# Softmax weights times values as three float32r products of high and low parts, the exponential taken twice

## The chip, the cores and the metric

The kernel runs on one NeuronCore of a Trainium2 chip. The metric is the device time of one execution in microseconds (us). Beside it stands the profile of one execution: for each engine (TensorE for matrix products, VectorE, ScalarE, GpSimd, and SyncE, which here only issues DMAs) the instructions with their start, their duration and what they waited for.

## The reference

One step of a one-layer hybrid encoder, for a prompt of 2048 tokens and for 8 streams of 16 new tokens with 512 cached ones. A combined input projection feeds two groups of heads: an SSD (state space) group and an attention group with forget gates. Their outputs go through one output projection, then a convolutional feed-forward network and a final norm. The change touches the attention of the prompt:

```python
def fox_block(q, k, v, fq, fk, q_pos, k_pos):
    s = jnp.einsum('bqhd,bkhd->bhqk', q, k).astype(jnp.float32) * FOX_SCALE
    s = s + (jnp.swapaxes(fq, 1, 2)[:, :, :, None] - jnp.swapaxes(fk, 1, 2)[:, :, None, :])
    s = jnp.where((k_pos[None, :] <= q_pos[:, None])[None, None], s, -jnp.inf)
    p = jax.nn.softmax(s, axis=-1)
    return jnp.einsum('bhqk,bkhd->bqhd', p.astype(v.dtype), v)
```

All is float32: 8 heads of 64 columns, 2048 queries and keys, causal.

## The kernel before, in words

The program has three phases that overlap. Phase A projects the input in four parts of 512 tokens (`a_body`, from L378). The attention runs over the same four parts of 512 queries and over 8 heads. Then come the output projection (`out_proj`, L910) and the feed-forward network (`ffn_part`), which take the second half of the time and are not touched, apart from `out_proj`.

TensorE's order is written out by hand (the `manual_schedule` block near the end of `hybrid_step`); the other engines' orders are chosen by the scheduler from its own times. The main loop there walks through the attention's blocks. After each block it gives out credit, and with it steps of the projection of the next part (stages 0 to 2) or of the output projection (stages 3 and 4); besides it runs the steps of a side job: the sample attention during part 0, SSD chunks (`ssd_chunk`) during parts 1 to 3. So each attention block on TensorE is followed by some us of other products.

Attention has two halves that run as a pipeline. `s_phase` (L653) computes scores with queries on partitions and takes their maxima (L668, L671), one head ahead. `t_phase` (L701) computes the scores again with keys on partitions, 128 keys by up to 512 queries a block: L728 and L729, both float32r products, and L731 for the mask on a diagonal block. ScalarE takes the exponential out of PSUM into the SBUF tile `pr` (L733), and two blocks later `weigh` (L695) multiplies it by the values (L696) into the PSUM tile `pv`. A part p has 8 heads of 4(p + 1) blocks, 320 in all; of the four blocks on the diagonal three are shorter (384, 256 and 128 queries).

L696 is a true float32 product. Its stationary operand, `vr` from `load_v` (L632), holds 64 columns of values and 64 columns of ones, so that one product gives the weighted sum and the softmax's denominator. For even heads the ones stand behind the values and for odd heads ahead of them. `end` copies both halves out of `pv` (L709, L710), and after two heads VectorE divides (`chores`: L713 in four pieces, L717).

Nearly everywhere else a float32 product is made of three float32r products. Float32r is a form of float32 in which a part of the digits is kept; `split` (L100) makes `hi`, the rounded number, and `lo`, what is left of it, and the product is hi x hi + hi x lo + lo x hi (`mm3`, L118).

The buffers that matter: PSUM tiles `s`, four of one bank each (`pss`), for the scores of both halves, the SSD chunks and the sample attention; one PSUM tile `pv`; three PSUM tiles `mm` for phase A; in SBUF five `pr`, three `v`, three `ks` (keys of `s_phase`), three `ev` (outputs of phase A on their way to memory), two `mx` (the split input of `out_proj`). SyncE issues all loads and stores but those of weights.

Of the kernel before, what the change touches and what calls it, by code (L numbers as in the profile page):

```python
# [8 lines left out]
F32 = mybir.dt.float32  # L9
# [8 lines left out]
P = 128  # L18
# [3 lines left out]
NB = 8  # L22
# [27 lines left out]
WB = 6  # L50
XB = 1
QB = 4
PB = 5
WA = 3
LEAD = 4

# [10 lines left out]
def hybrid_step(ctx: ExitStack, tc: tile.TileContext, i: dict, o: dict):  # L67
# [70 lines left out]
    def at(shape, tag, bufs, dt=F32):  # L138
        return ap_.tile(shape, dt, tag=tag, name=tag, bufs=bufs)
# [117 lines left out]
    def gates(p, dtf):  # L257
# [52 lines left out]
        V.tensor_copy(an[:, 0:8 * n].rearrange("p (c h) -> p c h", h=8), ct[:, 0, :, 0:8])  # L310
        pr = tpt()
        T.transpose(pr[0:8 * n, 0:P], an[:, 0:8 * n], ident)
        ar = at([40, P], "g_ar", 1)
        V.tensor_copy(ar[0:8 * n], pr[0:8 * n, 0:P])
        dS(ac_d[4 * p:4 * p + 4].rearrange("c h p -> (c h) p"), ar[0:32])
        if p == 0:
# [9 lines left out]
        for a in range(2):  # L326
            pr = tpt()
            for c in range(4):
                T.transpose(pr[0:8, c * P:(c + 1) * P], nh[:, a, c * 8:(c + 1) * 8].bitcast(F32), ident)
            fr = at([8, 512], "g_2k", 1)  # L330
            V.tensor_copy(fr, pr[0:8])
            dS(k2_d[:, 64 + a, p * 512:(p + 1) * 512], fr)
        yield
        if p > 0:
            return
# [16 lines left out]
        for c in range(4):  # L352
            V.scalar_tensor_tensor(snf[:, :, :, c], lcs[:, :, c, :], -1.0, cto, op0=ALU.mult, op1=ALU.subtract)
            V.tensor_add(cto, cto, ltt[:, :, c, :])
        snh = at([P, 2, 256], "g_2k", 1, F32R)
        split(snf.rearrange("p b h c -> p (b h c)"), snh[:, 0], snh[:, 1], V, V)
        yield
        pr = tpt()
        for a in range(4):
            T.transpose(pr[:, a * P:(a + 1) * P], snh[:, a // 2, (a % 2) * P:(a % 2 + 1) * P].bitcast(F32), ident)  # L360
        snr = at([P, 512], "xT", 2)
        V.tensor_copy(snr, pr)
        for a in range(4):
            dS(sf_d[a // 2, 4 * (a % 2):4 * (a % 2) + 4].rearrange("b h (c p) -> (b h c) p", p=P), snr[:, a * P:(a + 1) * P])
        ow8 = at([P, 8, NB], "g_ow8", 1)
        V.tensor_mul(ow8, cto.rearrange("p b h -> p h b"), blkb[:, None, :].to_broadcast([P, 8, NB]))
        ow = at([P, 8], "g_ow", 1)
        V.tensor_reduce(ow, ow8, op=ALU.add, axis=AX.X)
# [256 lines left out]
        return k12  # L625

    def load_ks(h, kb):
        ks = bt_([P, 512], "ks", 3, F32R)
        dma(ks[0:68].bitcast(F32), k2_d[h, :, kb * 512:(kb + 1) * 512])
        return ks  # L630

    def load_v(h, kb):  # L632

        vr = bt_([P, 4, P], "v", 3)
        e = h % 2 * HD
        G.memset(vr[:, :, HD - e:2 * HD - e], 1.0)
        dma(vr[:, :, e:e + HD], o["v"][4 * kb:4 * kb + 4, :, h * HD:(h + 1) * HD].rearrange("c p d -> p c d"))
        return vr

    def load_q(h, qb):  # L640
        q12 = bt_([P, 2, 512], "q12", QB, F32R)
# [51 lines left out]
    late, chores, exps = [], [], []  # L693

    def weigh(pv, vr, jj, of, pr, first, last, end):  # L695
        m = T.matmul(pv[:, of:512], vr[:, jj], pr[:, :512 - of], start=first, stop=last)  # L696
        pv_ins.append(m.ins)
        if last:
            end()

    def t_phase(h, qb, q12, yl, dn):  # L701

        pv = []
        order = [qb] + list(range(qb))

        def end():
            e = h % 2
            rs, ot = slice(e * 64, e * 64 + 64), slice(64 - e * 64, 128 - e * 64)
            S.copy(yl[rs], pv[0][rs])  # L709
            S.copy(dn[rs], pv[0][ot])  # L710
            if e:
                for a in range(4):
                    chores.append(lambda cc=slice(a * P, (a + 1) * P): V.reciprocal(dn[:, cc], dn[:, cc]))  # L713
                chores.append(norm)

        def norm():
            V.tensor_mul(yl, yl, dn)  # L717
            dS(mix_d[4 * qb:4 * qb + 4, :, 4 + h // 2, :].rearrange("c p t -> p c t"), yl.rearrange("p (c t) -> p c t", t=P))

        for kb in order:  # L720
            kk = load_k(h, kb)
            vr = load_v(h, kb)
            for jj in range(4):
                of = jj * P if kb == qb else 0
                W = 512 - of
                js = slice(jj * P, (jj + 1) * P)
                ps = pss()
                T.matmul(ps[:, :W], kk[:, 0, js], q12[:, 0, of:], start=True, stop=False)  # L728
                T.matmul(ps[:, :W], kk[0:68, 1, js], q12[0:68, 1, of:], start=False, stop=kb != qb)  # L729
                if kb == qb:  # L730
                    T.matmul(ps[:, 0:P], maskT, identb, start=False, stop=True)  # L731
                pr = bt_([P, 528], "pr", PB)
                exps.append(S.activation(pr[:, :W], ps[:, :W], AF.Exp).ins)  # L733
                first = kb == qb and jj == 0
                while len(late) >= (3 if late and late[0][0] == "first" else 2):
                    kind, a, x = late.pop(0)
                    if kind == "first":
                        a.append(psb.tile([P, 512], F32, tag="pv", name="pv", bufs=1))
                    weigh(a[0], *x)
                late.append(("first" if first else "", pv, (vr, jj, of, pr, first, kb == order[-1] and jj == 3, end)))  # L740
                yield
# [46 lines left out]
    def sample_attention():  # L788
# [33 lines left out]
        for b in range(NB):  # L822
# [38 lines left out]
            pT = bt_([P, 512], "pr", PB)  # L861
            S.copy(pT, pk)
            pk = pss()
            T.transpose(pk[0:NT, 0:P], pr[:, PAST:], ident)
            pt5 = bt_([NT, P], "bs", 1)
            V.tensor_copy(pt5, pk[0:NT, 0:P])
            yield
            pz = pss()
# [40 lines left out]

    def out_proj(c, after=None):  # L910
        mr = op.tile([P, KT, P], F32, tag="raw", name="raw", bufs=2)
        mx = op.tile([P, 2, KT, P], F32R, tag="mx", name="mx", bufs=2)

        for ks in ([slice(0, KT - 1), slice(KT - 1, KT)] if 12 <= c < 16 else [slice(0, KT)]):
            dA(mr[:, ks], mix_d[c][:, ks])
            split(mr[:, ks], mx[:, 0, ks], mx[:, 1, ks], S, V)
        y = op.tile([P, D], F32, tag="y", name="y", bufs=1)
        dA(y, i["xr"][c])
        ps = [pso.tile([P, 512], F32, tag="dn", name="dn") for _ in range(2)]

        def part(e, k):
            cc = slice(e * 512, (e + 1) * 512)
            T.matmul(ps[e], mx[:, 0, k], wo[k][:, 0, cc], start=k == 0, stop=False)  # L923
            T.matmul(ps[e], mx[:, 0, k], wo[k][:, 1, cc], start=False, stop=False)  # L924
            T.matmul(ps[e], mx[:, 1, k], wo[k][:, 0, cc], start=False, stop=k == KT - 1)  # L925
# [465 lines left out]
```

## Time and profile before

| | us |
|---|---|
| median of three runs | 3158.28 (3156.93 to 3160.4) |
| the profiled execution | 3159.18 |
| its span, first to last instruction | 3157.5 |
| mean granted clock of TensorE | 0.984 |

The profile's page lists busy time by engine, the chain of work that ended last, and groups of instructions by line, with the idle time of the engine ahead of them. A line of the kind `L733 ACT ACTIVATE pr<-s 128x512 ... x223 | 132.2, 595 | 202.3 <-PE s L729` says: line 733, ScalarE, reads `s` and writes `pr`, 223 times, busy 132.2 us together, 595 ns each, after 202.3 us in which ScalarE stood idle, mostly for TensorE. In the timeline the first number is the start and the second the duration, in us. A matmul's duration includes its way through the pipeline and its queue, so the time that one takes of TensorE is seen from start to start. A true float32 matmul leaves two records.

### The profile page before, as it was taken

The page shows a single profiled execution, that of the slowest core. Times are in us where ns is not written, and L with a number is a line of the kernel's source. Part 1 is how long each engine was busy: PE and PEld are TensorE (multiplying, and loading weights), DVE is VectorE, ACT ScalarE, POOL GpSimd, SP SyncE. Part 2 cuts the span into 40 slices and gives each one's busy share as a digit, 9 for nine tenths or more (in the row PEclk, how much of TensorE's full clock was granted, in tenths as well). Part 3 has the DMA queues.
Part 4 walks back from the last instruction along what each step waited for, and adds up shares of the span by engine and source line. Part 5 has one row for each costly group of instructions (what it writes and reads, how often), then busy time and mean ns, then how long its engine had stood idle before and what let it go on. Part 6 is the DMA issues. An engine that isn't in the chain of part 4 may idle for free.

```text
span 3157.5 us, 45849 instructions
## 1 busy us (share of the span) xinstructions
PE 3039.0 (96%) x17888; PEld 2682.1 (85%) x17888; DVE 1788.8 (57%) x3294; ACT 1066.7 (34%) x1927; POOL 865.8 (27%) x654
## 2 busy tenths in 40 slices
PE   7988998899999998999999999999999999999998
PEld 7886877787788775777899999999999999999998
DVE  4264466647565654543455555566555556766666
ACT  3343344444444444332322232233222223332322
POOL 3322322222222212000233232333223232433332
PEclk9998999899999999999999999999999999999999
DMA  4856675575556546445522121232121122322221
GB/s 123 247 174 202 200 244 158 181 223 165 162 155 204 153 132 187 161 148 181 171 67 67 54 69 61 72 116 79 61 67 61 60 67 83 105 67 81 74 69 65
DMA packets 233137, 395.77 MB, mean 125 GB/s; under 512 B 62544, under 2 KB 118488, under 8 KB 232920
## 3 DMA queue, kind: packets, MB, share of 16 engines
q1 hardware_dynamic: 181224, 238.41, 24.3%
q10 hardware_dynamic: 51696, 154.43, 15.8%
q8 instruction: 141, 2.31, 0.3%
q14 instruction: 76, 0.62, 0.1%
HBM read 314.51 MB, written 78.25 MB: 124 GB/s over the span
## 4 chain that ended last, share of the span: by engine, by line
PE 85%; DMA 8%; DVE 2%; ACT 2%; issue 1%; SPq 1%; POOL 1%; ACTq 0%; DVEq 0%; POOLq 0%
PE mm L120 11%; PE mm L121 11%; PE mm L122 11%; PE pv L696 6%; PE dn L1025 5%; PE dn L1026 5%; PE dn L1027 5%; PE mm L444 3%; PE mm L445 3%; PE mm L446 3%; DMA xt<-in_xr 2%; PE dn L923 2%; PE dn L925 2%; PE dn L924 2%; PE mm L397 2%; PE mm L399 2%
## 5 line engine op out<-in xcount | busy, mean ns | idle before, releaser
L105 POOL TENSOR_TENSOR wr<-raw,wr 128x1024 fp32r<-128x1024 f32 x198 | 476.5, 2415 | 1032.5 <-ACT wr L102 1024.5
L120 PE MATMUL mm<-nT,wr 128*128 128x386 f32 (+1 forms) x2112 | 696.4, 330 | 1.3 <-ACT wr L102 0.8
L121 PE MATMUL mm<-nT,wr 128*128 128x386 f32 (+1 forms) x2112 | 695.3, 329 | 0.1
L122 PE MATMUL mm<-nT,wr 128*128 128x386 f32 (+1 forms) x2112 | 694.4, 329 | 0.0
L1003 DVE SCALAR_TENSOR_TENSOR ac<-mm,cw,ac 128x384 f32<-128x384 f32 (+1 forms) x528 | 301.6, 571 | 344.8 <-ACT ac L1001 337.1
L1001 ACT ACTIVATE ac<-mm,cw 128x384 f32<-128x384 f32 (+1 forms) x264 | 172.7, 654 | 784.6 <-PE mm L122 784.0
L1028 DVE TENSOR_TENSOR y<-y,dn 128x512 f32<-128x512 f32 x374 | 255.0, 684 | 267.4 <-PE dn L1027 264.6
L121 PEld LDWEIGHTS mm<-nT,wr 128*128 128x128 f32 x2112 | 399.3, 189 | 6.8 <-DVE nT L105 0.3
L120 PEld LDWEIGHTS mm<-nT,wr 128*128 128x128 f32 x2112 | 397.5, 188 | 7.7 <-ACT wr L102 1.1
L122 PEld LDWEIGHTS mm<-nT,wr 128*128 128x128 f32 x2112 | 397.9, 188 | 5.7
L112 POOL TENSOR_TENSOR cmw<-craw,cmw 128x512 fp32r<-128x512 f32 (+1 forms) x192 | 248.6, 1317 | 467.8 <-ACT cmw L109 348.1
L444 PE MATMUL mm<-nT,cmw 128*128 128x256 f32 (+2 forms) x1024 | 309.7, 302 | 12.7 <-DVE cac L489 8.6
L671 DVE TENSOR_REDUCE nm<-s 128x1 f32<-128x512 f32 (+2 forms) x320 | 192.9, 607 | 198.6 <-PE s L668 114.1
L445 PE MATMUL mm<-nT,cmw 128*128 128x256 f32 (+2 forms) x1024 | 299.0, 292 | 0.0
L446 PE MATMUL mm<-nT,cmw 128*128 128x256 f32 (+2 forms) x1024 | 299.0, 292 | 0.0
L1025 PE MATMUL dn<-wr,ht 128*128 128x512 f32 x748 | 294.4, 394 | 2.9 <-DVE y L1028 1.7
L696 PE MATMUL pv<-pr,v 128*128 128x512 f32 (+3 forms) x640 | 293.5, 549 | 0.5 <-issue 0.5
L1026 PE MATMUL dn<-wr,ht 128*128 128x512 f32 x748 | 292.7, 391 | 0.0
L1027 PE MATMUL dn<-wr,ht 128*128 128x512 f32 x748 | 290.1, 391 | 0.0
L102 ACT CAST wr<-raw 128x1024 fp32r<-128x1024 f32 x198 | 203.2, 1042 | 174.1 <-PE dn L1027 161.4
L733 ACT ACTIVATE pr<-s 128x512 f32<-128x512 f32 (+1 forms) x320 | 169.3, 531 | 237.3 <-PE s L729 173.2
L668 PE MATMUL s<-ks,q 68*128 68x512 f32 (+2 forms) x320 | 199.8, 630 | 20.0 <-ACT pr L733 11.2
(294 smaller groups left out, 5174.9 us busy)
## 6 DMA issues: line engine op xcount, KB each, us to landing
raw<-in_w_up ACTq DMA_DIRECT2D x132, 512.0 KB
raw<-in_w_down ACTq DMA_DIRECT2D x66, 512.0 KB
craw<-in_w_cm ACTq DMA_DIRECT2D x64, 512.0 KB
k<-k_d SPq DMA_DIRECT2D x80, 256.0 KB
craw<-in_w_tm ACTq DMA_DIRECT2D x24, 512.0 KB
q_d<-qk SPq DMA_DIRECT2D x96, 128.0 KB
k_d<-qk SPq DMA_DIRECT2D x96, 128.0 KB
ks<-k_d SPq DMA_DIRECT2D x80, 136.0 KB
```

Of the source, the lines that this page charges most:

```text
L105: leng.tensor_sub(lo, src, hi.bitcast(F32))
L120: T.matmul(ps[:, :W], whi(k), wt[:, 0, k, :W], start=k == 0, stop=False)
L121: T.matmul(ps[:, :W], whi(k), wt[:, 1, k, :W], start=False, stop=False)
L122: T.matmul(ps[:, :W], wlo(k), wt[:, 0, k, :W], start=False, stop=k == n - 1)
L444: T.matmul(ps[:, :W], wc[:, 0, k, :], wk[:, 0], start=k == 0, stop=False)
L445: T.matmul(ps[:, :W], wc[:, 0, k, :], wk[:, 1], start=False, stop=False)
L446: T.matmul(ps[:, :W], wc[:, 1, k, :], wk[:, 0], start=False, stop=k == KT - 1)
L696: m = T.matmul(pv[:, of:512], vr[:, jj], pr[:, :512 - of], start=first, stop=last)
L1003: V.scalar_tensor_tensor(ac[:, 0:n], ps[:, j:j + n], cw2[:, ct, j:j + 1], ac[:, 0:n], op0=ALU.mult, op1=ALU.add)
L1025: T.matmul(ps, ht[:, 0, ts_], wd[:, 0, cc], start=x == 0, stop=False)
L1026: T.matmul(ps, ht[:, 0, ts_], wd[:, 1, cc], start=False, stop=False)
L1027: T.matmul(ps, ht[:, 1, ts_], wd[:, 0, cc], start=False, stop=x == len(g) - 1)
```

## The change

The softmax weights and the values are each split into a high and a low part, and L696 becomes three float32r products:

- ScalarE takes the exponential twice: once into `ph`, rounded to float32r, and once more in place in PSUM. VectorE subtracts `ph` from the second and so makes the low part `pl`.
- `load_v` loads the values into a tile `vw`, GpSimd copies them to the high part `vh` (64 columns of values, then 64 of ones, now for every head) and subtracts for the low part `vl` (64 columns).
- `weigh` multiplies `vh` by `ph`, `vl` by `ph` (64 rows of `pv` alone) and `vh` by `pl`.
- Room in SBUF: `pr` goes from five buffers to one, beside three each of `ph` and `pl`; `v` and `ks` go from three to two; `mx` is cut in halves, three of them in place of two whole ones; tiles of the gates (`g_ar`, `g_2k`, `g_ow8`) move onto `ev`; the sample attention's `pT` and `pt5` move onto `bs` and `cm`.

```diff
-PB = 5
+PB = 1
...
-            fr = at([8, 512], "g_2k", 1)
-            V.tensor_copy(fr, pr[0:8])
-            dS(k2_d[:, 64 + a, p * 512:(p + 1) * 512], fr)
+            for e in range(2):
+                fr = at([8, 256], "ev", 3)
+                V.tensor_copy(fr, pr[0:8, e * 256:(e + 1) * 256])
+                dS(k2_d[:, 64 + a, p * 512 + e * 256:p * 512 + (e + 1) * 256], fr)
...
-        ks = bt_([P, 512], "ks", 3, F32R)
+        ks = bt_([P, 512], "ks", 2, F32R)
...
-        vr = bt_([P, 4, P], "v", 3)
-        e = h % 2 * HD
-        G.memset(vr[:, :, HD - e:2 * HD - e], 1.0)
-        dma(vr[:, :, e:e + HD], o["v"][4 * kb:4 * kb + 4, :, h * HD:(h + 1) * HD].rearrange("c p d -> p c d"))
-        return vr
+        vh = bt_([P, 4, P], "v", 2, F32R)
+        vl = bt_([P, 4, HD], "vl", 2, F32R)
+        G.memset(vh[:, :, HD:].bitcast(F32), 1.0)
+        vw = bt_([P, 4, HD], "vw", 1)
+        dma(vw, o["v"][4 * kb:4 * kb + 4, :, h * HD:(h + 1) * HD].rearrange("c p d -> p c d"))
+        G.tensor_copy(vh[:, :, 0:HD], vw)
+        G.tensor_sub(vl, vw, vh[:, :, 0:HD].bitcast(F32))
+        return vh, vl
...
-        m = T.matmul(pv[:, of:512], vr[:, jj], pr[:, :512 - of], start=first, stop=last)
+        vh, vl = vr
+        ph, pl = pr
+        W = 512 - of
+        T.matmul(pv[:, of:512], vh[:, jj], ph[:, :W], start=first, stop=False)
+        T.matmul(pv[0:HD, of:512], vl[:, jj], ph[:, :W], start=False, stop=False)
+        m = T.matmul(pv[:, of:512], vh[:, jj], pl[:, :W], start=False, stop=last)
...
-            rs, ot = slice(e * 64, e * 64 + 64), slice(64 - e * 64, 128 - e * 64)
-            S.copy(yl[rs], pv[0][rs])
-            S.copy(dn[rs], pv[0][ot])
+            rs = slice(e * HD, (e + 1) * HD)
+            S.copy(yl[rs], pv[0][0:HD])
+            S.copy(dn[rs], pv[0][HD:])
...
-                pr = bt_([P, 528], "pr", PB)
-                exps.append(S.activation(pr[:, :W], ps[:, :W], AF.Exp).ins)
+                ph, pl = (bt_([P, 512], x, 3, F32R) for x in ("ph", "pl"))
+                S.activation(ph[:, :W], ps[:, :W], AF.Exp)
+                exps.append(S.activation(ps[:, :W], ps[:, :W], AF.Exp).ins)
+                V.tensor_sub(pl[:, :W], ps[:, :W], ph[:, :W].bitcast(F32))
+                pr = (ph, pl)
...
-        mx = op.tile([P, 2, KT, P], F32R, tag="mx", name="mx", bufs=2)
+        mx = [op.tile([P, 2, KT // 2, P], F32R, tag="mx", name="mx", bufs=3) for _ in range(2)]
...
-            split(mr[:, ks], mx[:, 0, ks], mx[:, 1, ks], S, V)
+            for x in range(2):
+                a, b = max(ks.start, 4 * x), min(ks.stop, 4 * x + 4)
+                if a < b:
+                    split(mr[:, a:b], mx[x][:, 0, a - 4 * x:b - 4 * x], mx[x][:, 1, a - 4 * x:b - 4 * x], S, V)
```

More of the change, by code (lines that the diff above doesn't have):

```diff
@@ L312, in gates @@
         T.transpose(pr[0:8 * n, 0:P], an[:, 0:8 * n], ident)
-        ar = at([40, P], "g_ar", 1)
+        ar = at([40, P], "ev", 3)
         V.tensor_copy(ar[0:8 * n], pr[0:8 * n, 0:P])
@@ L354, in gates @@
             V.tensor_add(cto, cto, ltt[:, :, c, :])
-        snh = at([P, 2, 256], "g_2k", 1, F32R)
-        split(snf.rearrange("p b h c -> p (b h c)"), snh[:, 0], snh[:, 1], V, V)
+        snh = [at([P, 256], "ev", 3, F32R) for _ in range(2)]
+        split(snf.rearrange("p b h c -> p (b h c)"), snh[0], snh[1], V, V)
         yield
@@ L359, in gates @@
         for a in range(4):
-            T.transpose(pr[:, a * P:(a + 1) * P], snh[:, a // 2, (a % 2) * P:(a % 2 + 1) * P].bitcast(F32), ident)
+            T.transpose(pr[:, a * P:(a + 1) * P], snh[a // 2][:, (a % 2) * P:(a % 2 + 1) * P].bitcast(F32), ident)
         snr = at([P, 512], "xT", 2)
@@ L364, in gates @@
             dS(sf_d[a // 2, 4 * (a % 2):4 * (a % 2) + 4].rearrange("b h (c p) -> (b h c) p", p=P), snr[:, a * P:(a + 1) * P])
-        ow8 = at([P, 8, NB], "g_ow8", 1)
+        ow8 = at([P, 8, NB], "ev", 3)
         V.tensor_mul(ow8, cto.rearrange("p b h -> p h b"), blkb[:, None, :].to_broadcast([P, 8, NB]))
@@ L860, in sample_attention @@
                 T.transpose(pk[:, c * P:(c + 1) * P], pr[:, c * P:(c + 1) * P], ident)
-            pT = bt_([P, 512], "pr", PB)
+            pT = bt_([P, 512], "bs", 1)
             S.copy(pT, pk)
@@ L864, in sample_attention @@
             T.transpose(pk[0:NT, 0:P], pr[:, PAST:], ident)
-            pt5 = bt_([NT, P], "bs", 1)
+            pt5 = bt_([NT, P], "cm", 1)
             V.tensor_copy(pt5, pk[0:NT, 0:P])
@@ L922, in part @@
             cc = slice(e * 512, (e + 1) * 512)
-            T.matmul(ps[e], mx[:, 0, k], wo[k][:, 0, cc], start=k == 0, stop=False)
-            T.matmul(ps[e], mx[:, 0, k], wo[k][:, 1, cc], start=False, stop=False)
-            T.matmul(ps[e], mx[:, 1, k], wo[k][:, 0, cc], start=False, stop=k == KT - 1)
+            T.matmul(ps[e], mx[k // 4][:, 0, k % 4], wo[k][:, 0, cc], start=k == 0, stop=False)
+            T.matmul(ps[e], mx[k // 4][:, 0, k % 4], wo[k][:, 1, cc], start=False, stop=False)
+            T.matmul(ps[e], mx[k // 4][:, 1, k % 4], wo[k][:, 0, cc], start=False, stop=k == KT - 1)
         with tc.issue_after(after) if after is not None else ExitStack():
```

## The prediction

> **What bounds the kernel now.** I read the page first, then the sums by stretch, then the matmuls by shape, then the timeline of a steady stretch, then the waits.
>
> ```profile
> span 3157.5 us, 45849 instructions
> ...
> PE 3039.0 (96%) x17888; PEld 2682.1 (85%) x17888; DVE 1788.8 (57%) x3294; ACT 1066.7 (34%) x1927; POOL 865.8 (27%) x654
> ...
> PE 85%; DMA 8%; DVE 2%; ACT 2%; issue 1%; SPq 1%; POOL 1%; ACTq 0%; DVEq 0%; POOLq 0%
> ```
>
> The chain that ended last (third line) is TensorE for 85% of the span, so a cut in TensorE time is worth having wherever TensorE is also the local bound. The sums by stretch (us; PE, PEld, DVE, ACT, POOL busy with instruction counts, then clock) say where that is:
>
> ```profile
> 500.00:600.00 100.00, 88.16 (x525) 73.02 (x525) 63.52 (x132) 38.61 (x82) 25.84 (x27) 0.93 0.61 188
> ...
> 700.00:800.00 100.00, 98.26 (x660) 81.26 (x659) 69.94 (x129) 47.21 (x101) 26.62 (x30) 0.98 0.55 163
> ...
> 1300.00:1400.00 100.00, 99.66 (x478) 72.44 (x476) 51.87 (x83) 34.64 (x73) 7.12 (x16) 1.00 0.47 154
> ```
>
> The values product (L696) runs in three stretches like these. From 700 us on TensorE has no slack, but VectorE is already at 52 to 70%.
>
> **TensorE: one float32 product becomes three float32r products.** The old product shows as two records per matmul, so 448 records are 224 matmuls of 512 columns; the diagonal blocks give 32 each of 384, 256 and 128.
>
> ```profile
> L696 PE MATMUL pv<-pr,v 128*128 128x512 f32 x448 | 238.1, 613 | 0.5 <-issue 0.5
> L696 PE MATMUL pv<-pr,v 128*128 128x384 f32 x64 | 27.2, 509 | 0.0
> L696 PE MATMUL pv<-pr,v 128*128 128x256 f32 x64 | 20.0, 394 | 0.0
> L696 PE MATMUL pv<-pr,v 128*128 128x128 f32 x64 | 13.5, 295 | 0.0
> ```
>
> These durations include queueing, so I take start-to-start times. One steady block of the last stage, of the timeline:
>
> ```profile
> 1386.75 0.40 PE L728 MATMUL s<-q,k 128*128 128x512 f32 x1
> 1386.99 0.40 PE L729 MATMUL s<-q,k 68*128 68x512 f32 x1
> 1387.22 1.02 PE L696 MATMUL pv<-pr,v 128*128 128x512 f32 x2
> 1387.48 0.60 ACT L733 ACTIVATE pr<-s 128x512 f32<-128x512 f32 x1 [2.16 <-PE s L729]
> 1387.68 0.80 PE L668 MATMUL s<-ks,q 68*128 68x512 f32 x1
> 1388.32 0.40 PE L923 MATMUL dn<-wo,mx 128*128 128x512 f32 x1
> ...
> 1389.25 0.39 PE L924 MATMUL dn<-wo,mx 128*128 128x512 f32 x1
> 1389.48 0.39 PE L925 MATMUL dn<-wo,mx 128*128 128x512 f32 x1
> 1389.70 0.39 PE L728 MATMUL s<-q,k 128*128 128x512 f32 x1
> ```
>
> A float32r product of 512 columns takes 0.23 us (1389.25, 1389.48, 1389.70). From L696's start to L923's is 1.10 us and holds one such product (L668), so the float32 product takes 0.87. Three of the new ones take 0.69: 0.18 saved, times 224 is 40.3 us. The second product has 64 stationary columns; it streams the same 512, so I give it the same time.
>
> ```profile
> 741.76 0.34 PE L728 MATMUL s<-q,k 128*128 128x384 f32 x1
> 741.93 0.34 PE L729 MATMUL s<-q,k 68*128 68x384 f32 x1
> 745.44 0.28 PE L728 MATMUL s<-q,k 128*128 128x256 f32 x1
> 745.56 0.28 PE L729 MATMUL s<-q,k 68*128 68x256 f32 x1
> 909.80 0.19 PEld L728 LDWEIGHTS s<-q,k 128*128 128x128 f32 x1 [1.58 <-ACT pr L733]
> 909.91 0.19 PEld L729 LDWEIGHTS s<-q,k 68*128 68x128 f32 x1
> ```
>
> At 384 columns: 0.87 x 3/4 = 0.65 against 3 x 0.17, saving 0.14 x 32 = 4.5. At 256: 0.435 against 0.36, 2.4. At 128 weight loads set a pace of 0.11: 0.22 against 0.33, a loss of 3.5. Together 43.7, taken as 44 us. The Trainium skill (FP8 and Floating Point Precision, TensorE Precision Notes) counts true float32 as four passes; a quarter off everywhere would save 0.22, 0.16, 0.11 and 0.05 a block, 59 us in all, and give 3133. The rows show each float32r product 12 ns over a quarter of 0.87, and the shortest blocks losing; I keep the rows.
>
> **ScalarE and VectorE.** Each block gets a second exponential, in place in PSUM, and a subtraction there.
>
> ```profile
> L671 DVE TENSOR_REDUCE nm<-s 128x1 f32<-128x512 f32 (+2 forms) x320 | 192.9, 607 | 198.6 <-PE s L668 114.1
> ...
> L733 ACT ACTIVATE pr<-s 128x512 f32<-128x512 f32 (+1 forms) x320 | 169.3, 531 | 237.3 <-PE s L729 173.2
> ```
>
> The second exponentials have L733's shapes and count: +169 us of ScalarE. The subtractions read one PSUM operand over the shapes and count of L671: +193 us of VectorE, 0.60 each. No row has ScalarE writing PSUM; I take L733's price, bounded by 0 and twice that for the write. Spread over the 1290 us of attention this is +13 and +15 points: neither engine becomes the bound by its sum (70 + 15 = 85% in the worst stretch). What counts is the order. The score tile comes from four PSUM buffers, `s`, shared with the maxima (L668) and the SSD chunks, and now goes back two steps later.
>
> Before, a tile is held from 1386.75 to 1388.08, 1.33 us. After: + 0.60 (exponential) + 0.69 (subtraction, the 512 form below) + two handovers of 0.09 (1387.39 to 1387.48) = 2.80. Per 2.95 us block (1386.75 to 1389.70) the program takes 2.4 tiles: scores, maxima, and 0.4 for an SSD chunk (six tiles, eight chunks in 128 blocks). Four tiles last 4.9 us, so the slack falls from 3.6 to 2.1 us. A block in step with its engines still costs TensorE nothing. A block that meets a long stretch on VectorE or ScalarE does (groups, then two lines of the timeline):
>
> ```profile
> L566 DVE TENSOR_TENSOR yt<-yt,s 128x512 f32<-128x512 f32 x17 | 11.7, 686 | 14.5 <-PE s L563 14.4
> L713 DVE RECIPROCAL rdb<-rdb 128x128 f32<-128x128 f32 x64 | 54.3, 910 | 22.2 <-ACT rdb L710 22.2
> L547 DVE TENSOR_TENSOR sg<-sg,bs 128x1024 f32<-128x1024 f32 x17 | 24.5, 1440 | 0.5 <-ACT sg L533 0.2
> L533 ACT ACTIVATE sg<-sg 128x1024 f32<-128x1024 f32 x17 | 17.9, 1052 | 0.2
> ...
> 744.53 3.38 DVE L713 RECIPROCAL rdb<-rdb 128x128 f32<-128x128 f32 x4
> ...
> 1399.09 2.45 ACT L532 ACTIVATE sg<-sg,acs 128x128 f32<-128x128 f32 x8 [1.01 <-DMA sg<-ac_d]
> ```
>
> There are 16 runs of four reciprocals (3.38 us), 17 of L532 with L533 (3.5 us) and 17 SSD runs around L547: 50 stretches of about 3.4 us. The block that arrives at the worst moment waits 3.4 and overruns the slack by 1.3: 50 x 1.3 = 65 us. One that arrives at a random moment overruns by 1.3 squared / (2 x 3.4) = 0.25: 12 us. I take 30, nearer the low end because 1300 to 1400 us, where blocks are densest, has VectorE at 52%.
>
> **GpSimd and the queues.** Each of 80 value loads now goes to a buffer of its own (`vw`) and GpSimd copies and subtracts it. Two groups, and between them a line of the waits (us in total, times, longest):
>
> ```profile
> L112 POOL TENSOR_TENSOR cmw<-craw,cmw 128x512 fp32r<-128x512 f32 x176 | 226.9, 1312 | 415.9 <-ACT cmw L109 308.6 <-issue 34.5 <-DMA k<-k_d 21.2
> ...
> POOL v L636 <- PE pv L696: 259.3, 49, 14.0
> ...
> L398 PE MATMUL mm<-cmw,nT 128*128 128x256 f32 x408 | 115.7, 284 | 1.3 <-POOL cmw L112 1.2
> ```
>
> Half of L112's 1.31 us each for copy and subtraction: 80 x 1.31 = 105 us on an engine at 7 to 27%. The copy waits for the load, and the weight halves (L112) queue behind it. GpSimd already stood 259 us for value buffers and TensorE lost 1.2 us to it, so I take 0; without that cover, a few us per stage, up to 8. The load issues on SP and now waits for the previous subtraction, with K loads behind it; a value buffer comes free two blocks into a group of four, so four blocks (some 12 us) cover the load and 1.3 us of GpSimd. Two instead of three `ks` and `v` buffers, halved `mx` tiles, and gate tiles moved onto `ev`: 0 to 6, I take 1. At the end of attention the last block's chain is longer by 0.60 + 0.69 + 0.18, about 2 us with the handover to the output projection.
>
> Sum: -44 + 30 + 1 + 2 = -11. The profiled execution took 3159.2 us (span 3157.5), 0.9 above the median of the three runs, 3158.3; 3159.2 - 11 = 3148.
>
> **Rivals.** (1) *PSUM tiles cost more than the products save: slower.* Its place is the four `s` tiles, its price the worst-case 65 us plus the 8 of GpSimd: -44 + 65 + 8 + 3 = +32, 3191. It decides from 41 us of waits on, 0.13 us per block. For it: VectorE at 70% before the +15 points between 700 and 800 us, and the waits of today (who waits for L733: us, times):
>
> ```profile
>   PEld s L668: 23.0, 12
> ```
>
> That is TensorE's loads waiting for the old exponential to give a tile back, with less than half the hold time. Against: the 3.6 us slack of the steady block. (2) *All of it is hidden:* the stretches fall where no tile is needed, -44 + 2 = 3117. For it: 85% is not a bound. Against: 500 to 600 us, where TensorE is busy 88% and shorter products partly become idle time. (3) *The clock.* That stretch also has clock 0.93 against 0.98 later. If the new waits brought 600 to 1480 us to 0.93, 880 x 0.05 / 0.93 = 47 us come on top of -11: 3195. The Trainium skill (TensorE: Matmul & The Clock Gate, A second HAM failure mode) describes this for cycling through PSUM. Against: waits are short, and 700 to 800 us holds 0.98. (4) *The products are not three cheap ones*, if the form runs as float32: L696 would not fall, 3 x 0.87 a block, +390 us. L728 and L729 are this form at 0.23, so I give it 1%.
>
> **Numbers.** Forecast case (part paid back, -6 to -30) 36%; waits about equal to the saving 18%; rival 1 31%; rival 2 9%; rival 3 5%; rival 4 1%. The range reaches from rival 2 to rival 1, 3117 to 3191, and leaves out the far ends. Faster by over 0.2% (6.3 us, about what can be told from no change): 36 + 9 = 45%; within it 18%; slower 31 + 5 + 1 = 37%.
>
> **What would show it.** L696 with three records per block at 0.23 us start to start and 0.69 in all; a second ACT row of 169 us in PSUM; a VectorE row near 193 us. My 30 us would stand in the waits of L728, L668 and the SSD matmuls on the new subtraction. If these exceed 41 us rival 1 holds; if they hardly appear, rival 2. Wrong altogether: waits on `vw`, `v` or `ev` of over 10 us, or a clock below 0.95 after 700 us.

## The result and the profile after

The changed kernel takes 3136.52 us in the median of four runs (3135.28 to 3141.62), the kernel before 3158.66 (3156.93 to 3160.4). The ratio is 0.9936, with a 95% interval of 0.9923 to 0.9948: 20 to 22 us faster, by the ratio or by the medians. The forecast was 3148, within 3117 to 3191.

The profiled execution after is the longest of its four (3141.62 us). Its page: span, busy time by engine, chain that ended last.

```profile
span 3139.9 us, 47419 instructions
...
PE 3014.7 (96%) x18208; PEld 2726.1 (87%) x18208; DVE 1946.4 (62%) x3639; ACT 1203.3 (38%) x2264; POOL 952.8 (30%) x814
...
PE 81%; DMA 8%; DVE 5%; ACT 3%; issue 1%; SPq 1%; POOL 1%; ACTq 0%; DVEq 0%; POOLq 0%
```

TensorE (PE) has 24 us less busy time than before and holds 81% of the last chain instead of 85%; VectorE's share of that chain went from 2% to 5%. VectorE gained 158 us of busy time, ScalarE 137, GpSimd 87. The place of the gain is seen in the first product of the feed-forward network (L120, an untouched line; instructions, then duration, then first and last start), before and after:

```profile
L120 PE MATMUL mm<-nT,wr x2112: 278/339/445, 1554.5 to 3135.2; 128*128 128x386 f32 x160, 128*128 128x258 f32 x32
```
```profile
L120 PE MATMUL mm<-nT,wr x2112: 278/340/442, 1538.2 to 3118.3; 128*128 128x386 f32 x160, 128*128 128x258 f32 x32
```

It starts 16.3 us earlier and its last start is 16.9 us earlier: all is won before 1550 us, and the second half runs as it did. The sums of the three stretches after:

```profile
500.00:600.00 100.00, 89.30 (x567) 78.21 (x566) 73.32 (x155) 47.48 (x104) 32.72 (x39) 0.95 0.61 188
700.00:800.00 100.00, 94.94 (x679) 83.00 (x678) 79.81 (x158) 58.24 (x130) 33.67 (x45) 0.98 0.57 164
1300.00:1400.00 100.00, 98.21 (x521) 77.84 (x520) 69.16 (x119) 51.47 (x114) 17.12 (x35) 1.00 0.50 160
```

VectorE (third busy number) is 10 to 17 points busier in each. TensorE, which had no slack at 700 and at 1300 us, now idles 5 and 2 us of 100 there. The clock did not fall in these three (0.95, 0.98, 1.00). It did in others, for one from 1100 to 1300 us, before and after:

```profile
1100.00:1300.00 200.00, 182.09 (x982) 135.18 (x980) 102.75 (x173) 80.61 (x166) 41.14 (x52) 0.96 0.53 160
```
```profile
1100.00:1300.00 200.00, 182.98 (x1028) 145.40 (x1028) 136.09 (x238) 108.49 (x232) 56.12 (x83) 0.93 0.54 163
```

The new instructions, by shape: three products, two exponentials (L742 into SBUF, L743 in place in PSUM), the subtraction (L744).

```profile
L703 PE MATMUL pv<-ph,v 128*128 128x512 f32 x224 | 98.5, 440 | 3.5 <-ACT ph L742 3.1 <-ACT rdb L719 0.4
L704 PE MATMUL pv<-ph,vl 128*64 128x512 f32 x224 | 91.0, 406 | 0.0
L705 PE MATMUL pv<-pl,v 128*128 128x512 f32 x224 | 91.4, 408 | 0.4 <-DVE pl L744 0.2
L742 ACT ACTIVATE ph<-s 128x512 fp32r<-128x512 f32 x224 | 133.2, 594 | 153.0 <-PE s L738 129.8 <-PE s L740 15.6 <-POOL cmw L112 4.2
L743 ACT ACTIVATE s<-s 128x512 f32<-128x512 f32 x224 | 132.8, 593 | 0.0
L744 DVE TENSOR_TENSOR pl<-s,ph 128x512 fp32r<-128x512 f32 x224 | 152.6, 682 | 30.7 <-ACT s L743 29.5
```

Timeline of the last stage after:

```profile
1368.82 0.68 DVE L105 TENSOR_TENSOR mx<-raw,mx 128x512 fp32r<-128x512 f32 x1
...
1369.42 0.68 DVE L675 TENSOR_REDUCE nm<-s 128x1 f32<-128x512 f32 x1
1369.64 0.39 PE L737 MATMUL s<-q,k 128*128 128x512 f32 x1
...
1370.02 0.68 DVE L744 TENSOR_TENSOR pl<-s,ph 128x512 fp32r<-128x512 f32 x1
1370.11 0.22 PE L703 MATMUL pv<-ph,v 128*128 128x128 f32 x1
...
1370.31 0.60 ACT L742 ACTIVATE ph<-s 128x512 fp32r<-128x512 f32 x1 [1.30 <-PE s L738]
1370.34 0.45 PE L672 MATMUL s<-ks,q 68*128 68x512 f32 x1
...
1370.62 0.60 PE L552 MATMUL s<-ident,xb 128*128 128x128 f32 x4
...
1370.80 0.59 ACT L743 ACTIVATE s<-s 128x512 f32<-128x512 f32 x1
...
1371.43 0.69 DVE L744 TENSOR_TENSOR pl<-s,ph 128x512 fp32r<-128x512 f32 x1
...
1372.92 0.40 PE L703 MATMUL pv<-ph,v 128*128 128x512 f32 x1
...
1373.15 0.39 PE L704 MATMUL pv<-ph,vl 128*64 128x512 f32 x1
...
1373.38 0.39 PE L705 MATMUL pv<-pl,v 128*128 128x512 f32 x1
...
1373.61 0.40 PE L672 MATMUL s<-ks,q 68*128 68x512 f32 x1
...
1373.85 0.39 PE L938 MATMUL dn<-wo,mx 128*128 128x512 f32 x1
```

A block of 128 columns in the kernel before, in the same stage:

```profile
1384.47 0.39 PE L696 MATMUL pv<-pr,v 128*128 128x128 f32 x2
...
1384.92 0.60 PE L551 MATMUL s<-ident,xb 128*128 128x128 f32 x4
```

Three things are to be seen. The three products of a full block take 0.23 us each (1372.92 to 1373.61 in 0.69); with the score product that follows (L672) it is 0.93 to the next one (1373.85), where the float32 product and the same score product took 1.10 (1387.22 to 1388.32 in the rows of the prediction). A 128-column block does not gain: with its score product it takes 0.51 (1370.11 to 1370.62), where it took 0.45 (1384.47 to 1384.92). The score tile written from 1369.64 is held until its subtraction ends at 1372.12: 2.48 us. And VectorE works through a queue: L105, L675 and L744 follow one another at 0.60 us (1368.82, 1369.42, 1370.02) although each is listed with 0.68. So durations of neighbours overlap, and the busy time added to an engine (158 us on VectorE, 137 on ScalarE) is less than the sum of its new rows.

Who on TensorE waited for the new subtraction, all six rows of the waits from 200 to 1480 us (us in total, times, longest):

```profile
PE s L737 <- DVE pl L744: 6.0, 4, 2.4
...
PE s L574 <- DVE pl L744: 2.9, 1, 2.9
...
PE s L593 <- DVE pl L744: 2.0, 1, 2.0
...
PE s L672 <- DVE pl L744: 1.7, 2, 1.3
...
PE pv L705 <- DVE pl L744: 0.2, 1, 0.2
...
PE s L537 <- DVE pl L744: 0.2, 1, 0.2
```

That is 13.0 us, where the forecast put 30, and almost nothing of it (0.2) is the third product waiting for its operand.

### The profile page after: what moved, and what is told of

The parts are those of the page before. It is cut to its first block, busy times and chain, and to the rows that moved or that the text cites. A ratio compares the mean times of both kernels' runs of the same rounds, so it can differ in the third digit from the quotient of the medians.

```text
span 3139.9 us, 47419 instructions
## 1 busy us (share of the span) xinstructions
PE 3014.7 (96%) x18208; PEld 2726.1 (87%) x18208; DVE 1946.4 (62%) x3639; ACT 1203.3 (38%) x2264; POOL 952.8 (30%) x814
## 4 chain that ended last, share of the span: by engine, by line
PE 81%; DMA 8%; DVE 5%; ACT 3%; issue 1%; SPq 1%; POOL 1%; ACTq 0%; DVEq 0%; POOLq 0%
PE mm L120 11%; PE mm L121 11%; PE mm L122 11%; PE dn L1040 5%; PE dn L1041 5%; PE dn L1042 5%; PE mm L445 3%; PE mm L446 3%; PE mm L447 3%; PE mm L398 2%; PE mm L399 2%; PE mm L400 2%; PE dn L938 2%; PE dn L939 2%; PE dn L940 2%; PE pv L703 2%
## 5 line engine op out<-in xcount | busy, mean ns | idle before, releaser
L105 POOL TENSOR_TENSOR wr<-raw,wr 128x1024 fp32r<-128x1024 f32 x198 | 476.7, 2415 | 1031.4 <-ACT wr L102 987.0
L120 PE MATMUL mm<-nT,wr 128*128 128x386 f32 (+1 forms) x2112 | 696.7, 330 | 0.5 <-ACT nT L102 0.5
L120 PEld LDWEIGHTS mm<-nT,wr 128*128 128x128 f32 x2112 | 397.8, 188 | 6.6 <-ACT nT L102 0.9
L445 PE MATMUL mm<-nT,cmw 128*128 128x256 f32 (+2 forms) x1024 | 310.4, 303 | 16.9 <-DVE cac L490 6.1
L675 DVE TENSOR_REDUCE nm<-s 128x1 f32<-128x512 f32 (+2 forms) x320 | 192.6, 604 | 111.7 <-PE s L674 59.1
L742 ACT ACTIVATE ph<-s 128x512 fp32r<-128x512 f32 (+1 forms) x320 | 169.8, 531 | 196.5 <-PE s L738 129.8
L744 DVE TENSOR_TENSOR pl<-s,ph 128x512 fp32r<-128x512 f32 (+1 forms) x320 | 192.3, 602 | 65.3 <-ACT s L743 59.7
L445 PEld LDWEIGHTS mm<-nT,cmw 128*128 128x128 f32 x1024 | 197.8, 193 | 23.7 <-ACT ev L465 6.8
```

What stands on the lines that cost most here:

```text
L105: leng.tensor_sub(lo, src, hi.bitcast(F32))
L120: T.matmul(ps[:, :W], whi(k), wt[:, 0, k, :W], start=k == 0, stop=False)
L445: T.matmul(ps[:, :W], wc[:, 0, k, :], wk[:, 0], start=k == 0, stop=False)
```

## The experiments

Two questions are open. How can about half of the 44 us have been given back when the waits on PSUM tiles show 13? And what did the edits for room do, which no row of the profile shows? All comparisons are over five rounds; "us" behind a ratio is the ratio's distance from 1 times 3158.5.

**Room edits and products apart.** `e1_room` is the kernel before with all the edits for room and nothing else: one exponential, one float32 product.

```diff
-                pr = bt_([P, 528], "pr", PB)
+                pr = bt_([P, 512], "ph", 3)
...
-        ks = bt_([P, 512], "ks", 3, F32R)
+        ks = bt_([P, 512], "ks", 2, F32R)
...
-        mx = op.tile([P, 2, KT, P], F32R, tag="mx", name="mx", bufs=2)
+        mx = [op.tile([P, 2, KT // 2, P], F32R, tag="mx", name="mx", bufs=3) for _ in range(2)]
```

> The kernel before with the float32 product and one exponential, but with all the room given up that the change gives up: two ks and two v buffers, three buffers for the exponential's output, gate tiles on ev, halved mx tiles, pT and pt5 moved. Theory (the 22 us given back are waits for the PSUM tiles s, held through the second exponential and the subtraction): no change, 3155 to 3162 us. Rival (the 22 us are the price of the buffers): 3173 to 3181 us.

Measured: 3143.3 us, ratio 0.9945 (0.9933 to 0.9957), 17 us faster. Neither expectation had that: most of what the whole change gains on balance is there without its products.

`e2_no_low` is the changed kernel without the second exponential and the subtraction.

```diff
-                ph, pl = (bt_([P, 512], x, 3, F32R) for x in ("ph", "pl"))
-                S.activation(ph[:, :W], ps[:, :W], AF.Exp)
-                exps.append(S.activation(ps[:, :W], ps[:, :W], AF.Exp).ins)
-                V.tensor_sub(pl[:, :W], ps[:, :W], ph[:, :W].bitcast(F32))
-                pr = (ph, pl)
+                ph = bt_([P, 512], "ph", 3, F32R)
+                exps.append(S.activation(ph[:, :W], ps[:, :W], AF.Exp).ins)
+                pr = (ph, ph)
```

> The changed kernel without the second exponential and without VectorE's subtraction; the third product multiplies the high part again, so the low part of the weights is left out of the result. TensorE has the same products. Theory (PSUM tiles held too long): the tile goes back after one exponential as before the change and the products' whole saving shows, 3112 to 3120 us. Rival (buffers, or GpSimd's split of the values): no gain against the change, 3133 to 3140 us.

Measured: 3117.49 us, 0.9867 (0.9851 to 0.9884), 42 us faster. Against `e1_room` the three products and the split of the values are worth 25 us by the ratios (from 17 faster to 42 faster). That is not all the TensorE time that they save: the pages show 3036.0 us of busy TensorE in `e1_room` and 2995.7 in `e2_no_low`, 40.3 less, but spans of 3142.7 and 3114.1, only 28.6 less. So 12 us of the saving became idle time. Against the changed kernel the second exponential and the subtraction cost 22 us by the ratios (0.9936 to 0.9867).

**Which room edit.** Each group of edits alone on the kernel before: `e5_mx` only the halved `mx`, `e6_ks_v` only two `ks` and two `v`, `e7_pr` only three weight tiles for five and the moved `pT` and `pt5`, `e8_ev` only the gate tiles on `ev`.

```diff
-        vr = bt_([P, 4, P], "v", 3)
+        vr = bt_([P, 4, P], "v", 2)
...
-            pT = bt_([P, 512], "pr", PB)
+            pT = bt_([P, 512], "bs", 1)
...
-        ow8 = at([P, 8, NB], "g_ow8", 1)
+        ow8 = at([P, 8, NB], "ev", 3)
```

> The kernel before with the output projection's mx tiles in halves alone. Theory (the 17 us that the room edits bring by themselves come from the finer mx halves where the output projection starts, 1100 to 1300 us): 3145 to 3152 us, with all of the gain after 1100 us. Rival (each edit only reshuffles the engines' orders, and no single one holds the gain): anything from 3145 to 3165 us, and the four parts do not add up to 17.

> The kernel before with two ks and two v buffers in place of three alone. Theory (fewer buffers cost a little, by later loads): 3158 to 3164 us. Rival (loads held back leave the SP queue and the DMA engines to others, and that is the gain of the room edits): 3142 to 3152 us, the gain in part 0.

> The kernel before with three buffers of their own for the exponential's output, one pr for the sample attention and the sample SSD chunk, pT on bs and pt5 on cm, alone. Theory (the sample attention no longer takes turns with the prompt's exponentials over the five pr buffers, which is where part 0 ends 8 us earlier in the run with all the room edits): 3147 to 3153 us, the gain in part 0. Rival (no single edit holds the gain): within 4 us of 3160.

> The kernel before with the gate tiles g_ar, g_2k and g_ow8 on the ev buffers alone. Theory (the gates' halved rows cost a copy and two stores more in each part, beside other work): 3158 to 3164 us. Rival (the stores through one g_2k buffer held VectorE 9 us, which three ev buffers take away, and that is the gain of the room edits): 3148 to 3154 us.

| | median us | ratio (95%) | us |
|---|---|---|---|
| e5_mx | 3160.74 | 0.9995 (0.9984 to 1.0007) | -2 |
| e6_ks_v | 3152.8 | 0.9977 (0.9966 to 0.9988) | -7 |
| e7_pr | 3154.66 | 0.9981 (0.997 to 0.9992) | -6 |
| e8_ev | 3150.75 | 0.9964 (0.9952 to 0.9976) | -11 |
| e1_room, all | 3143.3 | 0.9945 (0.9933 to 0.9957) | -17 |

Three of the four gain a little, and their sum (26) is more than the 17 of all together, so they are not terms that add. Taking a buffer away cannot shorten a wait for that buffer, and `e6_ks_v` does nothing else. `e8_ev` is another case, for its gate tiles get three buffers in place of one; it landed where its rival had put it (3148 to 3154), but not by the rival's mechanism: VectorE's copy of the gates waited 12.8 us for stores before (L331) and waits 22.6 for them in `e8_ev` (L332). All engines but TensorE have their order from the scheduler, and an edit to a buffer can change that order. The traces (operation and tile of each step, by start) show that it did for VectorE in `e5_mx`, `e7_pr` and `e8_ev`. In `e6_ks_v` ScalarE keeps its order, and one step of VectorE, one of GpSimd and a few loads of SyncE are all that changed places. So a new order is a candidate and not a cause that was shown. The granted clock is also higher with these edits (0.9870 against 0.9837 for the kernel before in the same group of runs; the last section), which goes with 6 to 10 of the 17 us. In the two profiled executions, though, the clock is nearly alike (0.984 and 0.985), and of 14.8 us of span 3.0 are busy time of TensorE (3039.0 and 3036.0) and 11.8 idle time. How much is the clock and how much shorter waits stays open, and so does why the edits do either.

**PSUM hold or load.** The forecast's theory was that the PSUM score tile comes back too late. The rival is that VectorE, busier, is later with everything it does for TensorE, whoever holds what. `e3_exp_sbuf` sends the second exponential to SBUF, so that the tile is free after it, and gives `pl` two buffers; `e4_once` takes one exponential out of PSUM, copies it in SBUF for the high part and subtracts there, so that the tile is held as short as before the change.

```diff
+                pf = bt_([P, 528], "pr", PB)
                 S.activation(ph[:, :W], ps[:, :W], AF.Exp)
-                exps.append(S.activation(ps[:, :W], ps[:, :W], AF.Exp).ins)
-                V.tensor_sub(pl[:, :W], ps[:, :W], ph[:, :W].bitcast(F32))
+                exps.append(S.activation(pf[:, :W], ps[:, :W], AF.Exp).ins)
+                V.tensor_sub(pl[:, :W], pf[:, :W], ph[:, :W].bitcast(F32))
```
```diff
+                pf = bt_([P, 528], "pr", PB)
-                S.activation(ph[:, :W], ps[:, :W], AF.Exp)
-                exps.append(S.activation(ps[:, :W], ps[:, :W], AF.Exp).ins)
-                V.tensor_sub(pl[:, :W], ps[:, :W], ph[:, :W].bitcast(F32))
+                S.activation(pf[:, :W], ps[:, :W], AF.Exp)
+                exps.append(S.copy(ph[:, :W], pf[:, :W]).ins)
+                V.tensor_sub(pl[:, :W], pf[:, :W], ph[:, :W].bitcast(F32))
```

> The changed kernel with the second exponential written to SBUF (two pr buffers, pl with two in place of three), so that the PSUM tile goes back after it and not after VectorE's subtraction: 0.78 us and VectorE's queue less. ScalarE and VectorE do as much as in the change. Theory (PSUM tiles held too long): half or more of the 22 us come back, 3118 to 3128 us. Rival (the load on VectorE and ScalarE as such, wherever the tiles lie): 3133 to 3140 us.

> One exponential from PSUM to SBUF, then ScalarE copies it to the high part and VectorE subtracts, both in SBUF: the PSUM tile is held as long as before the change, the engines have as many instructions as in the change. Theory (PSUM tiles held too long): nearly all of the 22 us come back, 3114 to 3124 us, at or below the run with the second exponential in SBUF. Rival (the load on VectorE and ScalarE as such): 3133 to 3140 us.

Measured: `e3_exp_sbuf` 3134.16 us, 0.9916 (0.9903 to 0.9928); `e4_once` 3137.23, 0.9932 (0.9916 to 0.9947). With the tile held as short as before, the time of `e4_once` is that of the changed kernel (0.9936), so a short hold alone brings nothing back. That does not yet clear the hold: with both operands in SBUF the subtraction loads VectorE more (1985.9 us by the page against 1946.4), and in `e4_once` the third product waits 17.6 us for `pl`, which has two buffers there. `e3_exp_sbuf` is 2 to 6 us lower, at intervals that touch; its waits moved to the third product, which now waits for an operand with two buffers instead of three:

```profile
PE pv L705 <- DVE pl L745: 12.5, 12, 2.5
```

So the smaller `pl` confounds both runs. `e3_exp_sbuf` is the fastest kernel here that computes everything, by no safe margin over the changed one.

**The two causes each alone.** `e9_vload` is `e2_no_low` plus a subtraction of `ph` from itself, in SBUF, into a tile that nobody reads: VectorE's load without the hold, the second exponential or an operand for TensorE to wait for. `e10_hold` is the other half: second exponential in PSUM and a subtraction that holds the tile, but of 32 columns only, with the third product reading `ph`.

```diff
+                exps.append(S.activation(ph[:, :W], ps[:, :W], AF.Exp).ins)
+                V.tensor_sub(pl[:, :W], ph[:, :W].bitcast(F32), ph[:, :W].bitcast(F32))
+                pr = (ph, ph)
```
```diff
-                V.tensor_sub(pl[:, :W], ps[:, :W], ph[:, :W].bitcast(F32))
-                pr = (ph, pl)
+                V.tensor_sub(pl[:, :32], ps[:, :32], ph[:, :32].bitcast(F32))
+                pr = (ph, ph)
```

> The run without exponential and subtraction (3117 us), with a subtraction of the same shapes put back on VectorE whose result nobody reads and which reads SBUF alone; the third product multiplies the high part again, so the low part of the weights is left out of the result. VectorE has its 190 us more, no PSUM tile is held for it and TensorE waits for none of it. Theory (the chain costs because PSUM tiles are held): 3114 to 3122 us. Rival (VectorE's load as such: maxima, evacuations and SSD steps all come later): 3128 to 3138 us.

> The changed kernel with the subtraction cut to 32 columns and the third product multiplying the high part again, so the low part of the weights is left out of the result. The PSUM tile is still held through the second exponential and a short VectorE step, but VectorE has some 130 us less. Theory (PSUM tiles held): 3126 to 3137 us. Rival (VectorE's load): 3115 to 3123 us.

Measured: `e9_vload` 3135.38 us, 0.9928 (0.9917 to 0.994); `e10_hold` 3121.4, 0.9885 (0.9872 to 0.9898). The load alone brings back 19 us of `e2_no_low`'s 42; the hold and ScalarE's exponentials bring back 4 to 6. Busy times up to the first product of the feed-forward network in `e2_no_low`, `e9_vload`, `e10_hold` and the changed kernel (PE, PEld, DVE, ACT, POOL; then the clock). TensorE works through the same matmuls, 9540 records, in each:

```profile
0.00:1512.37 1512.37, 1406.78 (x9540) 1226.23 (x9541) 825.57 (x1731) 602.29 (x1277) 457.63 (x565) 0.97 0.60 184
```
```profile
0.00:1531.96 1531.96, 1413.78 (x9540) 1229.26 (x9541) 1026.30 (x2051) 603.21 (x1277) 488.60 (x565) 0.97 0.60 182
```
```profile
0.00:1516.79 1516.79, 1415.38 (x9540) 1230.28 (x9541) 856.66 (x2050) 736.50 (x1597) 455.36 (x565) 0.97 0.60 183
```
```profile
0.00:1538.18 1538.18, 1425.89 (x9540) 1234.82 (x9541) 981.18 (x2051) 736.59 (x1597) 456.19 (x565) 0.96 0.59 181
```

With 201 us more on VectorE (`e9_vload`) the stretch is 19.6 us longer: TensorE stands idle for 12.6 of them, and is busy 7.0 us longer with the same products. With 134 us more on ScalarE, the hold and 31 us on VectorE (`e10_hold`) it is 4.4 us longer, and TensorE idles less than in `e2_no_low`. So VectorE's load alone can cost nearly as much as the whole chain costs in the changed kernel, and the hold alone cannot.

The changed kernel itself looks different. Its stretch is 25.8 us longer than that of `e2_no_low`, but only 6.7 of them are idle time of TensorE; in the other 19.1 it is busy with the same products for longer. The granted clock explains part of that: in the clock records of these traces it is either 1 or 0.5 of full speed, and in this stretch it is 0.5 for 96 us in `e2_no_low`, 99 in `e9_vload`, 102 in `e10_hold` and 126 in the changed kernel. Half of the busy time at half clock is 37.5 us in `e2_no_low` and 49.6 in the changed kernel, 12 of the 19. This profiled execution has the lowest clock of its four, so it overstates that share; the last section puts it at 5 to 8 of the 22 us from all runs.

The load in `e9_vload` does not cost in one place. TensorE's waits, all rows from 200 to 1480 us added up, are 73.7 us in `e2_no_low`, 84.7 in `e9_vload`, 70.0 in `e10_hold` and 78.0 in the changed kernel. (The rows that name VectorE alone are no measure of its load: they go from 24.5 to 42.4 us in `e9_vload`, but to 51.2 in `e10_hold`, which is 14 us faster: there VectorE is the last to give a score tile back, and the rows that name ScalarE fall from 39.8 to 8.7.) Some of the rows, first of `e2_no_low`, then of `e9_vload`:

```profile
PE s L589 <- DVE cm L583: 8.2, 1, 8.2
...
PE s L889 <- DVE zs L886: 1.5, 2, 0.7
...
PE s L689 <- DVE nm L675: 1.0, 1, 1.0
PE mm L445 <- DVE qk L462: 0.5, 1, 0.5
```
```profile
PE s L589 <- DVE cm L583: 8.5, 1, 8.5
PE s L689 <- DVE nm L675: 4.4, 1, 4.4
PE mm L445 <- DVE qk L462: 4.3, 2, 3.3
PE s L890 <- DVE zs L887: 4.1, 3, 2.6
...
PE s L672 <- DVE pl L743: 2.6, 1, 2.6
```

The maxima, the evictions of the projection (L462) and the sample attention all come later, each by a few us; the added step itself (L743) is named for 2.6. One caveat: the load in `e9_vload` is larger than in the changed kernel, 201 us of VectorE's page (1991.6 against 1790.9 in `e2_no_low`) beside 155 (1946.4), and GpSimd is slower there too (985.3 against 954.3). In proportion 155 us would cost 15, which with the 6 of `e10_hold` would give 21 of the 22. That is an estimate and not shown: the changed kernel's own trace has 6.7 us more idle time and not 15. What the runs show is that the load can cost this much; how the 22 us divide between the load, the hold and the clock stays open.

**Another engine for the subtraction.** `e11_gp_sub` is `e3_exp_sbuf` with the subtraction on GpSimd.

```diff
-                V.tensor_sub(pl[:, :W], pf[:, :W], ph[:, :W].bitcast(F32))
+                G.tensor_sub(pl[:, :W], pf[:, :W], ph[:, :W].bitcast(F32))
```

> The run with the second exponential in SBUF (3134 us), with the subtraction on GpSimd in place of VectorE; nothing is left out. Theory (PSUM tiles held): no nearer than that run, 3130 to 3137 us. Rival (VectorE's load): 3117 to 3126 us. A third case: GpSimd takes its work in order and stands at the value buffers up to 19 us at a time, so the low parts come late, 3140 us and more.

Measured: 3168.08 us, 1.0032 (1.0021 to 1.0044), slower than before the change. By shape, and who waited:

```profile
L745 POOL TENSOR_TENSOR pl<-pr,ph 128x512 fp32r<-128x512 f32 x224 | 296.9, 1330 | 159.7 <-ACT pr L744 148.3 <-PE pv L704 3.8 <-PE s L689 3.7
```
```profile
PE pv L705 <- POOL pl L745: 19.5, 13, 3.7
```

GpSimd takes 1330 ns for a full block, twice VectorE. Here a step of the chain itself is late.

**GpSimd's split of the values.** `e12_gp_values` is `e1_room` with the loads into `vw` and GpSimd's two steps, and one float32 product of the high values; the low part is left out of the product. Against the changed kernel:

```diff
+        m = T.matmul(pv[:, of:512], vh[:, jj].bitcast(F32), ph[:, :W], start=first, stop=last)
...
+                ph = bt_([P, 512], "ph", 3)
+                exps.append(S.activation(ph[:, :W], ps[:, :W], AF.Exp).ins)
+                pr = (ph, ph)
```

> The run with the room edits alone (3143 us) with the values loaded to vw and split by GpSimd as in the change, but one float32 product of the high part of the values with the single exponential, so the low part of the values is left out of the result. Theory (GpSimd's split costs TensorE nothing): 3139 to 3147 us. Rival (it is what eats the 18 us by which the products save less than their 44): 3152 to 3163 us.

Measured: 3145.22 us, 0.9965 (0.9952 to 0.9978), against 3143.3 and 0.9945 (0.9933 to 0.9957) of `e1_room`: 2 to 6 us, at overlapping intervals. The split costs little or nothing.

## Why the prediction was right or wrong

- **The products: right, a little high.** Each takes 0.23 us start to start. With the score product behind it, a full block went from 1.10 to 0.93 us in the rows shown, 0.17 saved; the medians over the blocks without idle time are 1.10 and 0.94. The 128-column blocks lose, as forecast, but 0.06 us each and not 0.11. TensorE's busy time fell 40.3 us (`e1_room` to `e2_no_low`) where the sum said 44. The Trainium skill's four passes (FP8 and Floating Point Precision, TensorE Precision Notes) would have given 59; this trace gives 0.69 against 0.87, not a quarter off.
- **Not all of it shortens the run: partly foreseen.** 25 us came out by the ratios (`e1_room` to `e2_no_low`), 28.6 in the profiled executions, of 40.3 of busy time. GpSimd's split may hold 2 to 6 of the rest; the others went into idle time, as rival 2's counter-argument said of the stretch from 500 to 600 us, where TensorE is still only 89% busy.
- **ScalarE and VectorE: right in the rows, high in the sum.** The subtractions' 192 us by rows are 155 to 158 us of busy time.
- **"What counts is the order. The score tile comes from four PSUM buffers": the mechanism failed.** The tile is held 2.48 us (forecast 2.80), yet the hold and the second exponential together cost 4 to 6 us (`e10_hold`), and a short hold, with a heavier subtraction, gains nothing (`e4_once`). The 30 us of that term are 22 measured. VectorE's load alone can cost 19 (`e9_vload`), spread over everything that VectorE owes TensorE; that it costs 15 of the 22 in the changed kernel is an estimate, and 5 to 8 go with a lower clock. The forecast looked only at blocks that meet a long stretch; it never priced the delay that the added 0.60 us put on the steps queued behind.
- **"`ks` and `v` buffers, halved `mx` tiles, and gate tiles moved onto `ev`: 0 to 6, I take 1": the term that was wrong.** The room edits gave 17 us (`e1_room`), and the three `ph` for five `pr` with the moved `pT` and `pt5`, which that sentence leaves out, gave 6 alone. The bound excluded a gain without a reason, on the view that fewer buffers can only wait longer.
- **GpSimd 0, up to 8: right** (`e12_gp_values`, 2 to 6 with overlap).
- **Signs of being wrong.** Two that the forecast named came. The clock was below 0.95 after 700 us: 0.93 from 1100 to 1300 us, in the shown row of the profiled execution. And VectorE waited 14.4 us for a buffer of `ev` to be stored (L332). The second sign could not tell much, since the same copy already waited 12.8 us for its one `g_2k` before; the first one belongs to the lower clock, which goes with 5 to 8 of the 22 us (last section).
- **Rivals.** Rival 1 did not happen here, but `e11_gp_sub` shows how near a slower kernel was: the same products with a slower subtraction end at +10 us, if by another mechanism. Rival 2's number, 3117, is that of `e2_no_low`, which lacks the chain. Rival 3 did not come in its size (0.98 from 700 to 800 us), but in small: over all runs the clock is 0.981 after and 0.983 before. Rival 4: L703 to L705 are three cheap ones.

The account by the ratios: room -17, products with the split of the values -25, second exponential and subtraction +22, together -20, the 0.9936 measured. Each term holds the clock that came with it. The forecast's -11 had -44 + 30 + 3: the products brought 19 us less than forecast, the second exponential and subtraction cost 8 less, and the edits for room gained 17 where 1 of cost was put. That these errors nearly cancel, so that 3136.5 lies within 12 us of 3148, is in part luck.

## What to carry to other kernels

A step added to an engine that is 60% busy is not free because nobody waits for that step: in `e9_vload` 201 us of it on VectorE cost 19 us, though TensorE needs none of its results. Where a scheduler sets the order of engines, bound an edit of buffers from both sides, and run it alone before crediting the main edit with the result. Waits added up by the engine that they name can mislead: compare TensorE's idle and busy time for the same products. To tell a held buffer from a loaded engine, build each alone: the load into a tile that nobody reads, and the hold with a step that is nearly empty.

## What the runs showed of the hardware

The granted clock moves with the kernel, and the time with it. Means over all runs of each kernel, worked out from the clock of every run:

| | runs | mean clock |
|---|---|---|
| before (all three groups of runs) | 55 | 0.9833 |
| e1_room | 5 | 0.9870 |
| e2_no_low | 4 | 0.9835 |
| after | 4 | 0.9810 |
| e9_vload | 5 | 0.9818 |
| e10_hold | 4 | 0.9830 |
| e11_gp_sub | 6 | 0.9770 |

Among 32 runs of the kernel before, where nothing differs but the run, a straight line through time and clock falls by 1.9 us for each 0.001; if TensorE alone made the time it would be 3.2 (a thousandth of 3158). At these two prices the clock goes with 6 to 10 of the 17 us of the room edits, with 5 to 8 of the 22 us between `e2_no_low` and the changed kernel, with 3 to 5 of the 19 us of `e9_vload`, and with 8 to 13 of the 31 us between the changed kernel and `e11_gp_sub`. Whether waiting lowers the clock or a lower clock lengthens the waits, these runs do not tell.

The subtraction of 512 columns takes 682 ns with one operand in PSUM, and 837 on average with both in SBUF. Each line by itself (duration least, median, most), in the changed kernel and in `e9_vload`:

```profile
L744 DVE TENSOR_TENSOR pl<-s,ph x320: 272/680/694, 172.6 to 1447.1; 128x512 fp32r<-128x512 f32 x128, 128x256 fp32r<-128x256 f32 x32
```
```profile
L743 DVE TENSOR_TENSOR pl<-ph x320: 270/684/2761, 172.3 to 1440.4; 128x512 fp32r<-128x512 f32 x128, 128x256 fp32r<-128x256 f32 x32
```

The medians agree, but the PSUM form never exceeds 694 ns, while the SBUF form reaches 2761. One of the long ones, in `e9_vload`, runs beside a GpSimd product of two SBUF tiles:

```profile
1365.26 1.04 POOL L558 TENSOR_TENSOR xe<-xd,te 128x512 f32<-128x512 f32 x1 [1.23 <-DVE xd L554]
...
1365.75 1.10 DVE L743 TENSOR_TENSOR pl<-ph 128x512 fp32r<-128x512 f32 x1
```

The Trainium skill (VectorE: DVE Perf Modes, Two Vector instructions with no wait between them) names the second SBUF read interface of VectorE as shared with GpSimd, and this row fits that: 1.10 us instead of 0.68 beside 0.55 us of overlap. The whole trace agrees. Of the 224 full subtractions in `e9_vload`, 125 have no GpSimd instruction beside them, and none of these takes over 694 ns; 99 overlap one, and they take 1027 ns on average, 58 of them over 700. In the changed kernel 95 of 224 overlap a GpSimd instruction, and none takes over 694. ScalarE's exponential takes the same time into SBUF and into PSUM, 594 and 593 ns.
